# Two-layer hybrid decoder trunk on one core: mixer projections as one 512-column product per weight tile, with the halves added outside TensorE

## Chip, cores and metric

One core of one Trainium2 chip (trn2). The metric is device time in microseconds of one execution of the whole program. Engines are called by the profile's names: PE is TensorE, PEld its weight loads, DVE VectorE, ACT ScalarE, POOL GpSimd, SP SyncE.

## What is computed

Two layers over x of 256 tokens by 1024 channels, float32. Each layer has a token mixer and a retrieval sublayer (PEER), each followed by a LayerNorm. Only the mixer's projections of x are touched:

```
proj = x @ w_in                       # 1024 -> 12 pieces: aq ak av | lx lg | rq rk rv rg | ga gb gc
aq, ak = rope(aq), rope(ak)           # dilated softmax attention, 3 groups of 4 heads
lx -> short conv -> RG-LRU;  y_b = h * gelu(lg)
rq, rk = rope(rq), rope(rk)           # retention, 4 heads;  y_c = silu(rg) * norm(ret)
merged = sigmoid(ga) * (y_a @ wb_a) + sigmoid(gb) * (y_b @ wb_b) + sigmoid(gc) * (y_c @ wb_c)
x = LayerNorm(alpha * x + merged @ w_out);  x = LayerNorm(alpha * x + peer(x))
```

## The kernel before

Float32 products are made of parts: every operand is split into a high part (a cast to float32r) and a low part (the rest), and `high*high + high*low + low*high` is accumulated in PSUM. x stands transposed in SBUF as `xh` and `xl`, eight tiles of 128 channels by 256 tokens each.

The weights are one stream of 408 tiles (128x1024) a layer, called jobs. `run` takes them in order: for job i it splits the tile of job i+2 (`ensure_split`: SP loads `raw`, ACT casts `wh` at L250, DVE and for some jobs POOL subtract to get `wl` at L259), writes the job's products (`body`), lets each waiting side generator take a step (`pump`), and then writes the job's `post`. Each engine carries out its instructions in this written order. Three tiles of `wh` and `wl` exist, so the splitting can be two jobs ahead of PE and no more. `pool_cols` gives POOL 640 of the 1024 columns of `wl` in the first 12 attention jobs of a layer and 256 in the other 12.

A layer's jobs: 8 `lx`, 12 `av`, 24 `aq`/`ak`, 32 retention jobs (16 of them `rq`/`rk`), 8 `lg`, 16 for gate and branch b, 12 for a, 16 for c, 8 for the output projection; then 16, 128 and 128 jobs of PEER, which the change leaves alone.

A "T" job makes a transposed output: 128 output channels on the partitions, 256 tokens in the columns. `mm_t` (L301 to L308) writes for each of 8 channel tiles a product of `wh` with `xh` (L304) and with `xl` (L305), then 8 of `wl` with `xh` (L307): 24 products of 256 columns into half of a PSUM bank `mm` (2 buffers). Two T jobs fill a bank; the post of the second reads it. In attention and retention the reader is `rope_qk`: two DVE products of the PSUM bank with the rotary tables (L641, L642) into `w2` tiles (6 buffers), then a POOL subtraction and addition (L643, L644) into `qk`, which PE reads for the scores (L660, L754) two jobs later.

Beside the attention jobs run the side generators: `lru2` (DVE reciprocals L576, POOL products L577 and L578, later DVE L582 and L583), `scores` (PE L660, DVE L663) and `att` (softmax, transposes, products with v).

Of the kernel before, what the change touches and what calls it, by code (L numbers as in the profile page):

```python
# [11 lines left out]
F32 = mybir.dt.float32  # L12
F32R = mybir.dt.float32r
# [156 lines left out]
def build(ctx: ExitStack, tc: tile.TileContext, I, out, layers=LAYERS, dbg=None):  # L170
# [10 lines left out]
    par = cp.tile([P, LAYERS, 8, 12], F32, name="par")  # L181
    csp = cp.tile([P, LAYERS, 8], F32, name="csp")
    mhalf = cp.tile([P, 2], F32, name="mhalf")
    xh = cp.tile([P, KT, S], F32R, name="xh")
    xl = cp.tile([P, KT, S], F32R, name="xl")

    uid = [0]

    def nm(s):
        uid[0] += 1  # L190
        return f"{s}_{uid[0]}"

    def mmps():
        return ps.tile([P, 512], F32, tag="mm", name=nm("mm"), bufs=2)
# [322 lines left out]
    def mixer(l, mp, xdram, xnext):  # L517
# [9 lines left out]
        def w2():  # L527
            return mp.tile([P, 512], F32, tag="w2", name=nm("w2"), bufs=6)
# [59 lines left out]
        def body_lx(job, h, lo):  # L588
            ct = job[2]
            q = ct % 2  # L590
            if q == 0:
                V["p"] = mmps()
            pt = V["p"]
            (mm_t2 if ct == 0 else mm_t)(pt[:, q * S:(q + 1) * S], h, lo, xh, xl)
            for c, dst, src in ((0, wg, I["wgate"][l]), (2, rope, I["rope"]), (4, mask, I["mask"])):
                if c == ct:
                    nc.sync.dma_start(dst, src)

            def post():
                lx = w2()  # L600
                nc.scalar.copy(lx, pt)
                add_side("lru", lru1(ct // 2, lx))
                if ct == 7:
                    V["lru2"] = add_side("lru", lru2())
            return post if q else None
# [27 lines left out]
        run(take(12), body_av, 1.4)  # L633

        def rope_qk(pt, dst, c, s):
            src = pt.rearrange("p (a t) -> p a t", a=2)
            t1 = w2()
            t2 = w2()
            t1v = t1.rearrange("p (a t) -> p a t", a=2)
            t2v = t2.rearrange("p (a t) -> p a t", a=2)  # L640
            nc.vector.tensor_tensor(t1v, src, rope[:, c:c + 1, :].to_broadcast([P, 2, S]), op=ALU.mult)  # L641
            nc.vector.tensor_tensor(t2v, src, rope[:, s:s + 1, :].to_broadcast([P, 2, S]), op=ALU.mult)  # L642
            nc.gpsimd.tensor_tensor(dst[:, 0, :], t1[:, 0:S], t2[:, S:2 * S], op=ALU.subtract)  # L643
            nc.gpsimd.tensor_tensor(dst[:, 1, :], t2[:, 0:S], t1[:, S:2 * S], op=ALU.add)  # L644
# [76 lines left out]
        def body_att(job, h, lo):  # L721
            name, (g, p, part) = job[1], job[2]
            if part == 0:
                V["p"] = mmps()
            pt = V["p"]
            mm_t(pt[:, part * S:(part + 1) * S], h, lo, xh, xl)

            def post():
                k = int(name == "ak")
                if k == 0:  # L730
                    V["qk"] = mp.tile([P, 2, 2, S], F32, tag="qk", name=nm("qk"), bufs=2)
                rope_qk(pt, V["qk"][:, k], 0, 1)
# [56 lines left out]
        def body_ret(job, h, lo):  # L789
            name = job[1]  # L790
            if name in ("rv", "rg"):
                hp, k2 = job[2], job[3]
                if k2 == 0:
                    V["acc"] = accps2()
                acc = V["acc"]
                mm_n(acc, h, lo, xh, xl, k2, k2 == 3)

                def post_n():
                    a = mp.tile([P, 2, 512], F32, tag="r4", name=nm("r4"), bufs=5)
                    V[name] = a  # L800
                    for t in range(2):
                        if name == "rv":
                            nc.scalar.copy(a[:, t, :], acc[t])
                        else:
                            th = w2()
                            nc.scalar.activation(th, acc[t], AF.Tanh, scale=0.5)
                            nc.vector.scalar_tensor_tensor(a[:, t, :], th, 1.0, acc[t], op0=ALU.add, op1=ALU.mult)
                return post_n if k2 == 3 else None
            hd, part = divmod(job[2], 2)
            if part == 0:  # L810
                V["p"] = mmps()
            pt = V["p"]
            mm_t(pt[:, part * S:(part + 1) * S], h, lo, xh, xl)

            def post():
                k = int(name == "rk")
                if k == 0:
                    V["qk"] = mp.tile([P, 2, 2, S], F32, tag="qk", name=nm("qk"), bufs=2)
                rope_qk(pt, V["qk"][:, k], 2, 3)
                if k:  # L820
                    add_side("ret", ret(hd, V["qk"], V["rv"], V["rg"]))
            return post if part else None
# [7 lines left out]
        def body_lg(job, h, lo):  # L830
            ct = job[2]
            q = ct % 2
            if q == 0:
                V["p"] = mmps()
            pt = V["p"]
            mm_t(pt[:, q * S:(q + 1) * S], h, lo, xh, xl)

            def post():
                ge = w2()
                nc.scalar.activation(ge, pt, AF.Gelu)  # L840
                d = slice(ct - 1, ct + 1)
                hv = V["h"][:, d, :]
                nc.vector.tensor_tensor(hv, hv, ge.rearrange("p (a t) -> p a t", a=2), op=ALU.mult)
                split_from(ybh[:, d, :], ybl[:, d, :], hv)
            return post if q else None
# [6 lines left out]
        def body_bc(job, h, lo):  # L852
            dt = job[2]
            if job[0] == "T":
                V["p"] = mmps()
                mm_t(V["p"][:, 0:S], h, lo, xh, xl)
                return None
            b = job[1]
            pt = V["p"]
            yh, yl = (ybh, ybl) if b == "b" else (ych, ycl)  # L860
            mm_t(pt[:, S:2 * S], h, lo, yh, yl)

            def post():
                tg = mp.tile([P, S], F32, tag="tg", name=nm("tg"), bufs=2)
                nc.scalar.activation(tg, pt[:, 0:S], AF.Tanh, scale=0.5)
                if b == "b":
                    nc.vector.scalar_tensor_tensor(mg[:, dt, :], tg, 1.0, pt[:, S:2 * S], op0=ALU.add, op1=ALU.mult)
                    return
                nc.vector.scalar_tensor_tensor(tg, tg, 1.0, pt[:, S:2 * S], op0=ALU.add, op1=ALU.mult)
                nc.vector.tensor_tensor(mg[:, dt, :], mg[:, dt, :], tg, op=ALU.add)  # L870
                split_from(V["mh"][:, dt, :], V["ml"][:, dt, :], mg[:, dt, :])
            return post

        def body_a(job, h, lo):
            if job[0] == "T":
# [12 lines left out]
            for q in range(2):
                mm_t(pa[:, q * S:(q + 1) * S], h, lo, yaT[:, 0], yaT[:, 1], n=4, base=q * 512)

            def post():
                d = slice(2 * job[2], 2 * job[2] + 2)
                tmp = V["tga"]
                nc.vector.scalar_tensor_tensor(tmp, tmp, 1.0, pa, op0=ALU.add, op1=ALU.mult)
                nc.gpsimd.tensor_tensor(mg[:, d, :], mg[:, d, :], tmp.rearrange("p (a t) -> p a t", a=2), op=ALU.add)
            return post
# [396 lines left out]
```

## Time and profile before

| | us |
|---|---|
| median of 3 runs (2526.70 to 2528.17) | 2526.88 |
| the profiled execution | 2526.77 |
| its span, first to last instruction | 2524.9 |
| PE busy | 2481.4 (98%) |
| DVE busy | 1834.6 (73%) |
| ACT busy | 1177.1 (47%) |
| POOL busy | 283.0 (11%) |
| mean granted TensorE clock | 0.996 |

Shares are averages over stages that have different limits, so the stages are read one by one below. Matmuls are pipelined: a row's own duration (0.28 us for 256 columns) is longer than the distance to the next one, and what a product costs in a row of products is that distance. A wait of PE on a weight part shows under PEld or PE with the engine that released it.

### The profile page before, as it was taken

To read this page: it belongs to the slowest core of one execution; us is meant where nothing else is said; L and a number is where in the kernel's file an instruction comes from. 1 tells how busy PE (TensorE), PEld (TensorE's weight loads), DVE (VectorE), ACT (ScalarE), POOL (GpSimd) and SP (SyncE) were. 2 spreads that over 40 slices of the span, in tenths; PEclk is the share of its full clock that TensorE was granted. 3 is DMA by queue.
4 is the path that set the end of the run, shared out by engine and by line. 5 is a ranking of instruction groups with operands and counts; after the bars stand their busy time and mean duration, and the time that the engine had idled before them with its cause. 6 is when DMAs were issued, how large, how long until landed. Compare 5 with 4: busy or idle time off the path is not lost.

```text
span 2524.9 us, 43400 instructions
## 1 busy us (share of the span) xinstructions
PE 2481.4 (98%) x17428; PEld 2301.5 (91%) x17428; DVE 1834.6 (73%) x2736; ACT 1177.1 (47%) x1480; POOL 283.0 (11%) x263
## 2 busy tenths in 40 slices
PE   8999999999999999999999999999999999999998
PEld 8989999899999988888789899989999999888886
DVE  7876656889888856765588766568888888566655
ACT  5444444444544444444454444444454444444443
POOL 0821110200000000000028220102000000000001
PEclk9999999999999999999999999999999999999999
DMA  6445566555556658776554455655555666577664
GB/s 236 154 148 164 167 203 201 190 175 171 184 193 200 193 196 259 227 229 226 169 206 154 155 170 165 209 183 180 175 181 176 197 195 198 197 257 228 227 226 135
DMA packets 165913, 485.96 MB, mean 192 GB/s; under 512 B 15056, under 2 KB 47952, under 8 KB 165072
## 3 DMA queue, kind: packets, MB, share of 16 engines
q1 hardware_dynamic: 119952, 434.43, 52.5%
q10 hardware_dynamic: 44800, 45.62, 5.6%
q8 instruction: 137, 2.24, 0.4%
q0 software_dynamic: 960, 3.15, 0.3%
q14 instruction: 64, 0.52, 0.1%
HBM read 462.16 MB, written 20.97 MB: 191 GB/s over the span
## 4 chain that ended last, share of the span: by engine, by line
PE 93%; DVE 4%; issue 1%; POOL 1%; ACT 1%; ACTq 0%; POOLq 0%; DVEq 0%
PE acc L1202 27%; PE mm L304 17%; PE mm L307 17%; PE mm L305 17%; PE acc L334 2%; PE acc L335 2%; PE acc L338 2%; PE acc L1128 1%; DVE wl L259 1%; PE acc L1129 1%; PE side L660 1%; PE side L970 0%; POOL wl L259 0%; PE side L716 0%; PE side L709 0%
## 5 line engine op out<-in xcount | busy, mean ns | idle before, releaser
L259 DVE TENSOR_TENSOR wl<-raw,wh 128x1024 fp32r<-128x1024 f32 (+3 forms) x817 | 1002.6, 1232 | 475.7 <-ACT wh L250 470.9
L250 ACT CAST wh<-raw 128x1024 fp32r<-128x1024 f32 (+1 forms) x817 | 850.2, 1048 | 565.8 <-PE acc L1202 346.9
L304 PE MATMUL mm<-xh,wh 128*128 128x256 f32 x3536 | 880.5, 287 | 0.7 <-ACT wh L250 0.7
L305 PE MATMUL mm<-xl,wh 128*128 128x256 f32 x3536 | 868.5, 283 | 0.0
L304 PEld LDWEIGHTS mm<-xh,wh 128*128 128x128 f32 x3536 | 678.8, 192 | 3.3 <-issue 2.0
L305 PEld LDWEIGHTS mm<-xl,wh 128*128 128x128 f32 x3536 | 679.6, 192 | 0.5
L1202 PE MATMUL acc<-wh,act 128*128 128x512 f32 x2016 | 539.3, 389 | 0.9 <-ACT act L342 0.9
L307 PE MATMUL mm<-xh,wl 128*128 128x256 f32 x3536 | 497.6, 283 | 5.6 <-DVE wl L259 4.0
L307 PEld LDWEIGHTS mm<-xh,wl 128*128 128x128 f32 x3536 | 456.6, 192 | 6.8 <-DVE wl L259 4.4
L1202 PEld LDWEIGHTS acc<-wh,act 128*128 128x128 f32 x2016 | 378.2, 188 | 79.9 <-ACT act L342 1.4
L1202 PE MATMUL acc<-wl,act 128*128 128x512 f32 x1008 | 310.2, 389 | 0.0
L1202 PEld LDWEIGHTS acc<-wl,act 128*128 128x128 f32 x1008 | 189.2, 188 | 39.3
L1171 ACT ACTIVATE ring<-mm 128x512 f32<-128x512 f32 x128 | 76.5, 598 | 188.2 <-PE mm L307 175.5
L259 POOL TENSOR_TENSOR wl<-raw,wh 128x640 fp32r<-128x640 f32 (+2 forms) x50 | 68.8, 1386 | 725.6 <-ACT wh L250 681.4
L1098 ACT ACTIVATE ge<-acc 128x512 f32<-128x512 f32 x64 | 38.4, 600 | 164.1 <-PE acc L1129 164.1
L376 POOL TENSOR_TENSOR lnv<-lnv,mhalf 128x1 f32<-128x1 f32 x8 | 5.6, 697 | 770.7 <-DVE lnv L378 765.4
L334 PE MATMUL acc<-wh,xh 128*128 128x512 f32 x224 | 91.4, 408 | 0.0
L343 DVE TENSOR_TENSOR act<-ring,act 128x512 fp32r<-128x512 f32 x128 | 87.7, 685 | 1.4 <-ACT act L342 1.4
L335 PE MATMUL acc<-wh,xl 128*128 128x512 f32 x224 | 87.6, 391 | 0.0
L342 ACT CAST act<-ring 128x512 fp32r<-128x512 f32 x128 | 78.7, 615 | 5.0 <-DVE ring L1104 4.2
L643 POOL TENSOR_TENSOR qk<-w,w 128x256 f32<-128x256 f32 x40 | 51.4, 1284 | 183.5 <-DVE w L642 151.1
L338 PE MATMUL acc<-wl,xh 128*128 128x512 f32 x224 | 69.1, 390 | 0.0
(253 smaller groups left out, 2329.1 us busy)
## 6 DMA issues: line engine op xcount, KB each, us to landing
raw<-in_ws SPq DMA_DIRECT2D x815, 512.0 KB, 3.4
gd<-ge ACTq DMA_DIRECT2D x64, 256.0 KB, 3.3
ring<-gd ACTq DMA_DIRECT2D x8, 2048.0 KB, 15.7
wg<-in_wgate SPq DMA_DIRECT2D x2, 1024.0 KB, 5.8
kk<-in_keys ACTq DMA_DIRECT2D x2, 1024.0 KB, 5.4
xd<-L POOLq DMA_DIRECT2D x8, 256.0 KB, 2.8
X<-xd ACTq DMA_DIRECT2D x2, 1024.0 KB, 5.8
dec<-in_dec ACTq DMA_DIRECT2D x2, 768.0 KB, 4.4
```

Source lines behind the costliest of these rows:

```text
L250: nc.scalar.copy(h[:, c], raw[:, c])
L259: eng.tensor_tensor(lo[:, c], raw[:, c], h[:, c].bitcast(F32), op=ALU.subtract)
L304: mm(o, lhsT=w, rhs=mh[:, koff + k, :], start=(k == 0), stop=False)
L305: mm(o, lhsT=w, rhs=ml[:, koff + k, :], start=False, stop=False)
L307: mm(o, lhsT=lo[:, base + k * P:base + (k + 1) * P], rhs=mh[:, koff + k, :], start=False, stop=(k == n - 1))
L334: mm(acc[t], lhsT=sh[:, k, ts], rhs=h[:, q * 512:(q + 1) * 512], start=first, stop=False)
L335: mm(acc[t], lhsT=sl[:, k, ts], rhs=h[:, q * 512:(q + 1) * 512], start=False, stop=False)
L338: mm(acc[t], lhsT=sh[:, k, ts], rhs=lo[:, q * 512:(q + 1) * 512], start=False, stop=(last and q == 1))
L342: nc.scalar.copy(h, src)
L343: nc.vector.tensor_tensor(lo, src, h.bitcast(F32), op=ALU.subtract)
L1171: nc.scalar.activation(ring[s][:, i - 1:i + 1, :], pt.rearrange("p (a t) -> p a t", a=2), AF.Gelu)
L1202: mm(V["y"][t][n], lhsT=a[:, part, q, ts], rhs=w[:, n * 512:(n + 1) * 512], start=(j == 0 and x == 0), stop=False)
```

## The change

`xh` and `xl` become two halves of one tile `xx`, so that for each channel tile their 2 x 256 columns lie side by side. `mm_w` takes the place of `mm_t` in the T jobs of x (all but the first two `lx` jobs of a layer): 8 products of `wh` with 512 columns (high part of x in the first half of the output, low part in the second), then 8 of `wl` with 256 columns into the first half. The two halves of the output are added afterwards by `addhalves`: an ACT copy of the second half to SBUF (L325) and a DVE addition of the first half (L326). A pair of T jobs now takes a two-bank tile `acc`, which had been used by the "N" jobs alone (2 buffers). What had read PSUM now reads the sum in SBUF. For gates b and c the sum and the tanh are written in the T job's own post, and the branch product goes to a `side` bank.

```diff
-    xh = cp.tile([P, KT, S], F32R, name="xh")
-    xl = cp.tile([P, KT, S], F32R, name="xl")
+    xx = cp.tile([P, KT, 2, S], F32R, name="xx")
+    xh, xl = xx[:, :, 0, :], xx[:, :, 1, :]
...
+    def mm_w(o, h, lo, both, n=KT, base=0):
+        for k in range(n):
+            mm(o, lhsT=h[:, base + k * P:base + (k + 1) * P], rhs=both(k), start=(k == 0), stop=False)
+        for k in range(n):
+            mm(o[:, 0:S], lhsT=lo[:, base + k * P:base + (k + 1) * P], rhs=both(k)[:, 0, :], start=False,
+               stop=(k == n - 1))
+    def xboth(k):
+        return xx[:, k]
+    def addhalves(dst, pt):
+        v = pt.rearrange("p (a f t) -> p a f t", a=2, f=2)
+        nc.scalar.copy(dst, v[:, :, 1, :])
+        nc.vector.tensor_tensor(dst, dst, v[:, :, 0, :], op=ALU.add)
...
         def rope_qk(pt, dst, c, s):
-            src = pt.rearrange("p (a t) -> p a t", a=2)
+            src = w2().rearrange("p (a t) -> p a t", a=2)
+            addhalves(src, pt)
...
         def body_att(job, h, lo):
-                V["p"] = mmps()
+                V["p"] = accpair()
-            mm_t(pt[:, part * S:(part + 1) * S], h, lo, xh, xl)
+            mm_w(pt[:, part * 512:(part + 1) * 512], h, lo, xboth)
...
             def post():
                 ge = w2()
-                nc.scalar.activation(ge, pt, AF.Gelu)
+                addhalves(ge.rearrange("p (a t) -> p a t", a=2), pt)
+                nc.scalar.activation(ge, ge, AF.Gelu)
...
         def body_bc(job, h, lo):
             if job[0] == "T":
-                V["p"] = mmps()
-                mm_t(V["p"][:, 0:S], h, lo, xh, xl)
-                return None
+                pt = mmps()
+                mm_w(pt, h, lo, xboth)
+                def post_g():
+                    tg = mp.tile([P, S], F32, tag="tg", name=nm("tg"), bufs=3)
+                    nc.scalar.copy(tg, pt[:, S:512])
+                    nc.vector.tensor_tensor(tg, tg, pt[:, 0:S], op=ALU.add)
+                    nc.scalar.activation(tg, tg, AF.Tanh, scale=0.5)
+                    V["tg"] = tg
+                return post_g
-            pt = V["p"]
+            pt = sideps()[:, 0:S]
-            mm_t(pt[:, S:2 * S], h, lo, yh, yl)
+            mm_t(pt, h, lo, yh, yl)
```

The jobs of `lx` (from the third), `rq`/`rk`, `lg` and `ga` are changed like those of `aq`/`ak`. In the built program of both layers 1248 products of 512 columns and 1248 of 256 stand for 3744 of 256, that is for 156 jobs: 12 `lx`, 48 `aq`/`ak`, 32 `rq`/`rk`, 16 `lg`, 48 gates. DVE has 94 instructions more (62 of 512 columns, 32 of 256), ACT 88 more; POOL and SP have as many as before.

DVE in the attention stage of the first layer, before (`wl` are weight parts, L663 the scores, L641 and L642 the rotary products):

```order
L259 TENSOR_TENSOR wl_924<-raw_742,wh_923 128x384
L576 RECIPROCAL L_114_762<-L_114_762 128x256
L259 TENSOR_TENSOR wl_959<-raw_849,wh_958 128x384
L663 SCALAR_TENSOR_TENSOR sm_987<-side_989,mask_129 128x384
L663 SCALAR_TENSOR_TENSOR sm_988<-side_990,mask_129 128x384
L641 TENSOR_TENSOR w_148_1002<-mm_928,rope_128 128x512
L642 TENSOR_TENSOR w_149_1003<-mm_928,rope_128 128x512
L259 TENSOR_TENSOR wl_1011<-raw_884,wh_1010 128x384
```

The same place in the changed program:

```order
L259 TENSOR_TENSOR wl_852<-raw_757,wh_851 128x384
L594 RECIPROCAL L_114_716<-L_114_716 128x256
L259 TENSOR_TENSOR wl_879<-raw_790,wh_878 128x384
L688 SCALAR_TENSOR_TENSOR sm_899<-side_901,mask_128 128x384
L688 SCALAR_TENSOR_TENSOR sm_900<-side_902,mask_128 128x384
L326 TENSOR_TENSOR w_150_914<-w_150_914,acc_856 128x512
L666 TENSOR_TENSOR w_151_917<-w_150_914,rope_127 128x512
L667 TENSOR_TENSOR w_152_918<-w_150_914,rope_127 128x512
L259 TENSOR_TENSOR wl_926<-raw_817,wh_925 128x384
```

One addition stands ahead of the rotary products, and these read `w` (SBUF) where they read `mm` (PSUM).

DVE in gate and branch b, before (L867 multiplies the gate with the branch product):

```order
L259 TENSOR_TENSOR wl_3178<-raw_3075,wh_3177 128x1024
L259 TENSOR_TENSOR wl_3209<-raw_3111,wh_3208 128x1024
L867 SCALAR_TENSOR_TENSOR L_480_3110<-tg_3236,mm_3181 128x256
L259 TENSOR_TENSOR wl_3242<-raw_3142,wh_3241 128x1024
L259 TENSOR_TENSOR wl_3273<-raw_3175,wh_3272 128x1024
L867 SCALAR_TENSOR_TENSOR L_480_3110<-tg_3300,mm_3245 128x256
```

And in the changed program:

```order
L887 TENSOR_TENSOR tg_2890<-tg_2890,mm_2873 128x256
L259 TENSOR_TENSOR wl_2897<-raw_2808,wh_2896 128x1024
L899 SCALAR_TENSOR_TENSOR L_500_2748<-tg_2890,side_2900 128x256
L259 TENSOR_TENSOR wl_2929<-raw_2835,wh_2928 128x1024
L887 TENSOR_TENSOR tg_2949<-tg_2949,mm_2932 128x256
```

An addition of 256 columns (L887) stands between the weight parts of the T job and of the branch job.

## Rows read from the trace of the kernel before

**Rows 1.** The page, its parts 1 and 4: busy time of PE, and the chain that ended last by engine.

```profile
PE 2481.4 (98%) x17428; PEld 2301.5 (91%) x17428; DVE 1834.6 (73%) x2736; ACT 1177.1 (47%) x1480; POOL 283.0 (11%) x263
...
PE 93%; DVE 4%; issue 1%; POOL 1%; ACT 1%; ACTq 0%; POOLq 0%; DVEq 0%
```

**Rows 2.** Busy time by stretch (start:end, its length, then busy us and instructions of PE, PEld, DVE, ACT, POOL; granted clock; DMA). In order: the `lx` jobs, the attention jobs from the first L577 to the last third, the softmax part of attention, retention, `lg`, the gates and branches, all of layer 0; then `lx` and attention of layer 1.

```profile
5.75:34.09 28.34, 27.20 (x201) 26.49 (x202) 22.61 (x52) 15.78 (x23) 1.98 (x2) 1.00 0.88 316
79.64:120.86 41.22, 40.16 (x336) 38.02 (x335) 35.23 (x39) 14.31 (x14) 40.67 (x39) 1.00 0.49 162
120.86:143.90 23.04, 20.50 (x156) 19.96 (x155) 20.28 (x27) 10.93 (x17) 14.52 (x14) 0.93 0.44 145
...
158.44:268.38 109.94, 109.75 (x719) 98.50 (x717) 73.04 (x104) 45.94 (x63) 23.21 (x21) 1.00 0.49 161
268.38:294.84 26.46, 26.46 (x217) 26.20 (x215) 18.39 (x27) 14.89 (x21) 3.03 (x3) 1.00 0.44 139
294.84:420.92 126.08, 126.08 (x1059) 126.08 (x1057) 70.03 (x80) 55.50 (x72) 8.93 (x4) 1.00 0.62 202
1259.87:1290.66 30.79, 27.51 (x202) 25.39 (x202) 28.00 (x30) 17.14 (x27) 17.52 (x14) 0.99 0.62 229
1328.80:1412.63 83.83, 81.32 (x668) 78.42 (x666) 70.12 (x89) 35.84 (x45) 62.23 (x59) 1.00 0.47 158
```

**Rows 3.** Timeline of PE in an attention T job (start, length, what): its first product, its last eight, and the first of the next job.

```profile
98.85 0.28 PE L304 MATMUL mm<-xh,wh 128*128 128x256 f32 x1
...
100.77 1.12 PE L307 MATMUL mm<-xh,wl 128*128 128x256 f32 x8
101.73 0.28 PE L304 MATMUL mm<-xh,wh 128*128 128x256 f32 x1
```

**Rows 4.** Timeline of PE in PEER's last product: 512-column products in the same split form.

```profile
950.12 1.07 PE L1202 MATMUL acc<-wh,act 128*128 128x512 f32 x4
951.03 0.61 PE L1202 MATMUL acc<-wl,act 128*128 128x512 f32 x2
```

**Rows 5.** Timeline of POOL in the attention stage, one period of two jobs.

```profile
97.88 1.56 POOL L259 TENSOR_TENSOR wl<-raw,wh 128x640 fp32r<-128x640 f32 x1
99.41 1.05 POOL L577 TENSOR_TENSOR L<-L,L 128x256 f32<-128x256 f32 x1
100.55 0.74 POOL L578 TENSOR_TENSOR L<-L,L 128x256 f32<-128x256 f32 x1
101.25 1.88 POOL L259 TENSOR_TENSOR wl<-raw,wh 128x640 fp32r<-128x640 f32 x1
103.10 0.73 POOL L643 TENSOR_TENSOR qk<-w,w 128x256 f32<-128x256 f32 x1
103.80 1.05 POOL L644 TENSOR_TENSOR qk<-w,w 128x256 f32<-128x256 f32 x1
104.81 1.54 POOL L259 TENSOR_TENSOR wl<-raw,wh 128x640 fp32r<-128x640 f32 x1
```

**Rows 6.** Timeline of DVE at the same time.

```profile
98.21 1.65 DVE L259 TENSOR_TENSOR wl<-raw,wh 128x384 fp32r<-128x384 f32 x1
99.79 0.68 DVE L641 TENSOR_TENSOR w<-mm,rope 128x512 f32<-128x512 f32 x1
100.39 0.68 DVE L642 TENSOR_TENSOR w<-mm,rope 128x512 f32<-128x512 f32 x1
100.99 0.72 DVE L259 TENSOR_TENSOR wl<-raw,wh 128x384 fp32r<-128x384 f32 x1
...
103.29 0.96 DVE L259 TENSOR_TENSOR wl<-raw,wh 128x384 fp32r<-128x384 f32 x1
```

**Rows 7.** Groups of DVE by line and shape from 79.64 to 120.86 us (count, busy us, mean ns, idle before).

```profile
L259 DVE TENSOR_TENSOR wl<-raw,wh 128x384 fp32r<-128x384 f32 x9 | 9.9, 1096 | 0.5 <-ACT wh L250 0.5
...
L641 DVE TENSOR_TENSOR w<-mm,rope 128x512 f32<-128x512 f32 x7 | 4.8, 679 | 0.0
L642 DVE TENSOR_TENSOR w<-mm,rope 128x512 f32<-128x512 f32 x6 | 4.1, 677 | 0.0
```

**Rows 8.** The same from 172.8 to 200 us, where POOL is busy for a tenth of the time.

```profile
L259 DVE TENSOR_TENSOR wl<-raw,wh 128x1024 fp32r<-128x1024 f32 x8 | 9.8, 1221 | 3.7 <-ACT wh L250 3.6
...
L582 DVE SCALAR_TENSOR_TENSOR L<-L,L 128x256 f32<-128x256 f32 x2 | 0.8, 419 | 0.0
L641 DVE TENSOR_TENSOR w<-mm,rope 128x512 f32<-128x512 f32 x1 | 0.7, 689 | 0.0
...
L343 DVE TENSOR_TENSOR yaT<-side,yaT 128x256 fp32r<-128x256 f32 x1 | 0.4, 425 | 2.6 <-ACT yaT L342 2.6
```

**Rows 9.** The same from 120.86 to 158.44 us, with POOL busy about half of the time.

```profile
L582 DVE SCALAR_TENSOR_TENSOR L<-L,L 128x256 f32<-128x256 f32 x4 | 3.3, 820 | 0.0
```

**Rows 10.** Groups of ACT from 5 to 34 us: what a read of PSUM costs it.

```profile
L601 ACT COPY w<-mm 128x512 f32<-128x512 f32 x3 | 1.7, 582 | 2.7 <-PE mm L307 2.7
...
L558 ACT ACTIVATE w<-side,par 128x256 f32<-128x256 f32 x2 | 0.9, 475 | 4.7 <-PE side L556 4.7
```

**Rows 11.** Waits from 79.64 to 120.86 us (who, for whom: total us, times, longest).

```profile
ACT wh L250 <- PE mm L305: 14.8, 6, 4.2
...
PEld mm L307 <- POOL wl L259: 1.0, 2, 0.7
```

**Rows 12.** A stretch of two us behind the longest stop of PE in attention: length, PE busy, granted clock, DMA.

```profile
134.00:136.00 2.00, 1.73 (x8) 0.50 0.75 250
```

More of the change, by code (lines that the diff above doesn't have):

```diff
@@ L591, in body_lx @@
             if q == 0:
-                V["p"] = mmps()
+                V["p"] = mmps() if ct == 0 else accpair()
             pt = V["p"]
-            (mm_t2 if ct == 0 else mm_t)(pt[:, q * S:(q + 1) * S], h, lo, xh, xl)
+            if ct < 2:
+                (mm_t2 if ct == 0 else mm_t)(pt[:, q * S:(q + 1) * S], h, lo, xh, xl)
+            else:
+                mm_w(pt[:, q * 512:(q + 1) * 512], h, lo, xboth)
             for c, dst, src in ((0, wg, I["wgate"][l]), (2, rope, I["rope"]), (4, mask, I["mask"])):
@@ L600, in post @@
                 lx = w2()
-                nc.scalar.copy(lx, pt)
+                if ct < 2:
+                    nc.scalar.copy(lx, pt)
+                else:
+                    addhalves(lx.rearrange("p (a t) -> p a t", a=2), pt)
                 add_side("lru", lru1(ct // 2, lx))
@@ L810, in body_ret @@
             if part == 0:
-                V["p"] = mmps()
+                V["p"] = accpair()
             pt = V["p"]
-            mm_t(pt[:, part * S:(part + 1) * S], h, lo, xh, xl)
+            mm_w(pt[:, part * 512:(part + 1) * 512], h, lo, xboth)
             def post():
@@ L833, in body_lg @@
             if q == 0:
-                V["p"] = mmps()
+                V["p"] = accpair()
             pt = V["p"]
-            mm_t(pt[:, q * S:(q + 1) * S], h, lo, xh, xl)
+            mm_w(pt[:, q * 512:(q + 1) * 512], h, lo, xboth)
             def post():
                 ge = w2()
-                nc.scalar.activation(ge, pt, AF.Gelu)
+                addhalves(ge.rearrange("p (a t) -> p a t", a=2), pt)
+                nc.scalar.activation(ge, ge, AF.Gelu)
                 d = slice(ct - 1, ct + 1)
@@ L854, in body_bc @@
             if job[0] == "T":
-                V["p"] = mmps()
-                mm_t(V["p"][:, 0:S], h, lo, xh, xl)
-                return None
+                pt = mmps()
[7 more added lines that the diff above has]
+                return post_g
             b = job[1]
-            pt = V["p"]
+            pt = sideps()[:, 0:S]
             yh, yl = (ybh, ybl) if b == "b" else (ych, ycl)
-            mm_t(pt[:, S:2 * S], h, lo, yh, yl)
+            mm_t(pt, h, lo, yh, yl)
+            tg = V["tg"]
             def post():
-                tg = mp.tile([P, S], F32, tag="tg", name=nm("tg"), bufs=2)
-                nc.scalar.activation(tg, pt[:, 0:S], AF.Tanh, scale=0.5)
                 if b == "b":
-                    nc.vector.scalar_tensor_tensor(mg[:, dt, :], tg, 1.0, pt[:, S:2 * S], op0=ALU.add, op1=ALU.mult)
+                    nc.vector.scalar_tensor_tensor(mg[:, dt, :], tg, 1.0, pt, op0=ALU.add, op1=ALU.mult)
                     return
-                nc.vector.scalar_tensor_tensor(tg, tg, 1.0, pt[:, S:2 * S], op0=ALU.add, op1=ALU.mult)
+                nc.vector.scalar_tensor_tensor(tg, tg, 1.0, pt, op0=ALU.add, op1=ALU.mult)
                 nc.vector.tensor_tensor(mg[:, dt, :], mg[:, dt, :], tg, op=ALU.add)
@@ L877, in body_a @@
                 if dt % 2 == 0:
-                    V["pg"] = mmps()
+                    V["pg"] = accpair()
                 q = dt % 2
                 pt = V["pg"]
-                mm_t(pt[:, q * S:(q + 1) * S], h, lo, xh, xl)
+                mm_w(pt[:, q * 512:(q + 1) * 512], h, lo, xboth)
                 def post_g():
                     V["tga"] = w2()
-                    nc.scalar.activation(V["tga"], pt, AF.Tanh, scale=0.5)
+                    addhalves(V["tga"].rearrange("p (a t) -> p a t", a=2), pt)
+                    nc.scalar.activation(V["tga"], V["tga"], AF.Tanh, scale=0.5)
                 return post_g if q else None
```

## The prediction

> **What bounds the kernel now.** I read the page first, then busy time by stretch, then timelines of single engines. PE is busy for 98% of the span and holds 93% of the chain that ended last [rows 1], so time is mostly PE's. The stretches say where not [rows 2]. In `lg` and in the gates PE is busy all of the time, in retention 109.75 of 109.94 us, and DVE has some third of each free: PE alone bounds these. In the attention stretch from 79.64 to 120.86 us, PE is busy 40.16 of 41.22 us, but POOL is busy 40.67 us too and DVE 35.23: two engines are full at once, and a third nearly. In the softmax part DVE has 20.28 of 23.04 us and PE waits. In layer 1's `lx` DVE has 28.00 of 30.79 us.
>
> The reader is to see in the POOL timeline that it never rests: each row begins where the one before ended [rows 5]. One period of two jobs, from 97.88 to 104.81, takes 6.93 us: a weight part of 640 columns, L577, L578, a weight part, L643, L644. Where undisturbed, a 256-column row takes 0.73 and a 640-column one 1.54, so that the six sum to 2 x 1.54 + 4 x 0.73 = 6.0 us. The missing 0.9 us is in rows that are longer than their like (1.05 for 0.73, 1.88 for 1.54), each beside a DVE weight part. On DVE the same shows from the other side: the 384-column part that takes 0.72 at 100.99 takes 1.65 at 98.21 and ends 0.4 us after POOL's row does [rows 5, 6]. Two engines seem to pass one door in turn. Not every DVE row pays: the rotary products L641 and L642 take 679 and 677 ns in the POOL-full stretch and L641 689 ns where POOL is nearly idle [rows 7, 8]. L582, with two inputs in SBUF, takes 419 ns there and 820 on average beside POOL [rows 8, 9]. So DVE rows with two SBUF inputs pay beside POOL, rows with one input in PSUM do not.
>
> **PE, products.** 24 products of 256 columns lie 2.88 us apart from job to job, 0.120 us each (98.85 to 101.73, and eight of L307 from 100.77 to 101.73) [rows 3]. 512-column products of the same parts lie (951.03 - 950.12) / 4 = 0.2275 us apart [rows 4]. A changed job takes 8 x 0.2275 + 8 x 0.120 = 2.78 us, 0.10 less. 156 jobs: 15.6 us, 48 of them in attention (4.8), 12 in `lx` (1.2), 96 elsewhere (9.6). That is all that the change can give.
>
> A rule of the Trainium skill makes this smaller: "TensorE: Matmul & The Clock Gate", section "Back-to-back issue gap", gives columns / 2.4 + 2.5 ns for an isolated product, by which one of 512 saves 2.5 ns on two of 256, and the whole change 1248 x 2.5 ns = 3.1 us. The rows, 0.120 and 0.2275, are both above that formula, and their difference is the larger saving; I go by the rows.
>
> **ACT, copies.** 62 copies of 512 columns at 582 ns, six of them in place of copies that stood there, and 32 of 256 at no more than 475 ns [rows 10]: some 48 us in both layers. ACT has half of each stretch free [rows 2], so the work costs nothing; if that cover went, the weight casts behind it would come late. What counts is latency: about 0.6 us more between the last product and its reader.
>
> **DVE, additions.** 62 of 512 columns with one input in PSUM: 0.68 us each, as L641; 32 of 256 at 425 ns (L343) [rows 7, 8]. In the gates that is 13.6 us of 252 in two layers, with PE full and DVE at 70 of 126 us: nothing. In `lg`, ga and retention (2.7, 2.7 and 5.4 us a layer) nothing either. At the end of `lg`, copy and addition put 1.3 us before the branch input; the next T job's 2.78 us and the first half of the b job's products cover it. The tanh of gates b and c moves ahead of the branch product, out of the wait; no gain, as PE waited for neither.
>
> **Attention.** A rope pays three times on DVE: the addition (0.68, or 0.60 from start to start [rows 6]), and two products that now read two SBUF inputs. No row of before shows these. Bounds: nothing, as L641 beside POOL now; or a wait for a whole POOL row each, 0.73 to 1.54 us [rows 5]. At the lower bound the 12 additions of a layer (7.2 us) fit into DVE's rest. At the upper one, with 0.73, a rope takes 0.60 + 2 x 0.73 = 2.06 us on DVE, 24.7 us a layer, less the rest of 8.8 us (6.0 and 2.8 in the two stretches [rows 2]): 16 us. The nearest rows are the L259 and L582 ones, and I take their price: the door is held by each product for as long as its columns take, (1221 - 425) / 768 = 1.04 ns a column [rows 8], 0.53 us, 1.07 us a rope, and DVE waits 0.40 us each (820 - 419).
> - From 79.64 to 120.86: POOL has no rest, so what the door gives to DVE it takes from POOL, and with it from the weight parts that PE waits for (1.0 us already [rows 11]). Six ropes x 1.07 = 6.4 us. PE's own gain there is lost, since PE then waits.
> - From 120.86 to 143.90: POOL has rests, DVE is near full. Four ropes at 0.60 + 2 x 0.40 = 1.4 us: 5.6 us, less DVE's rest of 2.76: 2.8 us.
> - The last two ropes: 0.2 us gained on PE, as much lost; nothing.
>
> 9.2 us a layer. Layer 1's attention has about the same load (POOL 62.23 us, after 40.67 and 14.52 in layer 0's two stretches) [rows 2]: 18.4 us in both.
>
> "SBUF — State Buffer", section "Who interferes with whom", in the Trainium skill says that a VectorE instruction with two SBUF inputs contends with a GpSimd one that reads SBUF, that one with at most one does not, and that the later blocks until the earlier is through. The rows agree for L582 and L641; that it holds for a product with the broadcast rotary table, no run here shows. By it a whole POOL row can be waited out, which is the upper bound above.
>
> **`lx`.** Three additions a layer. Layer 0 has DVE rest (22.61 of 28.34) and PE's 0.6 us gain goes there: nothing. In layer 1, 3 x 0.68 = 2 us meet a rest of 2.79 us, part of it waits that cannot be moved: 1 us lost.
>
> **Sum.** -9.6 + 18.4 + 1.0 = +9.8 us on the profiled execution's own 2526.77 us: 2536.6. The median of the runs is 0.1 us above that execution; I say **2537 us**.
>
> **The rivals.**
> 1. *TensorE decides everywhere: faster.* In the POOL-full stretch ACT's casts still wait 14.8 us for PE [rows 11], so PE sets the pace there as well, and a part of POOL's busy time may be waiting. It decides if POOL can give up 1.07 us a rope without PE noticing. Against it: PE does wait for POOL's weight part [rows 11], and no POOL row starts late [rows 5]. Then all of 15.6 us come, or 9.6 with attention unchanged: 2511 to 2518 us.
> 2. *The losses only eat the gain: no change.* The door is taxed as said, but PE stops no more than 4 to 6 us a layer, since DVE's rest takes in the additions: -9.6 + 8 to 12 + 1: 2526 to 2531 us.
> 3. *The scores come late as well.* Before, L642 ended at 101.07 and POOL came to L643 at 103.10: 2.0 us to spare [rows 5, 6]. Copy (0.58), addition (0.60) and two waits (0.40 each) take 2.0 us. If it is more, POOL stands before L643 with the weight parts behind it, and PE before the scores. At 1.3 us for six scores a layer: 16 us more, 2553 us. A long stop also brings PE's clock down, as the half rate behind the softmax stop shows [rows 12].
> 4. *The wide product saves nothing*, if it takes as long as two narrow ones: 9.6 us less gain, 2546 us. [rows 4] speak against it with 512-column products of the same type.
>
> The formula of the clock-gate page above would put the saving near this case.
>
> **How the numbers follow.** Two levels count as different here when they are over 0.2% (5 us) apart, about what a measurement can tell. My forecast has 0.52: attention loses 6 to 16 us a layer (the upper bound), 2530 to 2550, nearly all of it slower. Rival 1 has 0.18, faster. Rival 2 has 0.15, and with a little of the forecast's lower end makes the middle 0.17. Rival 3 has 0.12 and rival 4 0.03, both slower. Slower: 0.65. The range leaves out rival 1 (0.18) and little else: it goes from 2520, between rivals 1 and 2, to 2555, behind rival 3.
>
> **What would show it.** The gate jobs 2.78 us apart where 2.88 stood, and the wide products 0.2275 apart (rival 4: 0.240). Rotary products of attention at about 1.0 us on average and the additions at 0.68 (rival 1: all 0.68). The attention stage some 9 us longer, with POOL without rest for longer and PE waiting for `wl` of POOL and DVE; retention, `lg` and gates 1.6, 0.8 and 2.4 us shorter. In rival 3, waits of POOL L643 on DVE inside the full stretch, and PE on `qk`. I would be wrong if attention kept its length, which would say that POOL's full row of instructions did not set PE's pace.

## The result: slower, by twice the forecast and for two reasons

| | before | changed |
|---|---|---|
| median of 6 runs, us | 2527.53 (2526.09 to 2528.41) | 2547.43 (2546.22 to 2550.84) |
| span of the profiled execution, us | 2524.9 | 2544.7 |

The ratio is 1.0081, 95% interval 1.0068 to 1.0094: 19.9 us slower. Forecast was slower, 2537 us, in a range from 2520 to 2555; the loss is twice the 9.8 us that the sum gave.

The page of the changed kernel, its parts 1 and 4, answers to [rows 1]:

```profile
PE 2483.3 (98%) x16180; PEld 2241.0 (88%) x16180; DVE 1906.6 (75%) x2830; ACT 1215.0 (48%) x1568; POOL 292.4 (11%) x263
...
PE 85%; DVE 7%; ACT 3%; POOL 2%; issue 2%; DMA 0%; ACTq 0%; SPq 0%; POOLq 0%; DVEq 0%
```

PE still looks busy for 98%, yet its part of the chain that ended last fell from 93% to 85%. Most of the 8 points went to DVE, ACT and POOL: PE waits for them, in stops that are mostly short (the longest new one, for softmax rows of DVE, has 4.2 us where 2.1 was the longest before).

Where they lie is told by the distance between the first products of the stages' first jobs, in both traces (layer 0, layer 1; us against before):

| stage | forecast, each layer | layer 0 | layer 1 |
|---|---|---|---|
| `lx` | 0, +1.0 | -0.3 | -0.2 |
| attention | +9.2 | +7.5 | +6.3 |
| retention | -1.6 | -0.9 | -0.9 |
| `lg` | -0.8 | +1.0 | +1.0 |
| gate and branch b | -0.8 | +0.8 | +0.8 |
| a | -0.8 | -0.7 | -0.7 |
| c | -0.8 | +1.4 | +1.4 |
| output projection | 0 | +1.9 | +1.0 |

All that follows is within 0.1 us. The last row is to be read with care: the output projections of the two layers differ by 0.46 us in the kernel before already, and by as much from run to run where nothing was changed near them. Attention lost less than was forecast; `lg`, b, c and the output projection, which were to gain 2.4 us a layer, lost 5.1 and 4.2. Busy time by stretch of the changed kernel, columns as in [rows 2]: the second half of attention, retention, `lg`, b, a, c, output projection of layer 0:

```profile
115.81:166.02 50.21, 44.52 (x252) 38.19 (x251) 45.65 (x56) 22.76 (x35) 30.42 (x30) 0.93 0.43 141
166.02:275.06 109.04, 108.75 (x591) 91.74 (x590) 79.11 (x112) 50.59 (x71) 25.30 (x21) 1.00 0.51 162
275.06:302.53 27.47, 26.48 (x152) 22.87 (x150) 20.10 (x30) 16.30 (x25) 3.06 (x3) 1.00 0.40 134
302.53:349.42 46.89, 46.02 (x320) 42.93 (x321) 28.01 (x36) 24.42 (x37) 0.00 (x0) 1.00 0.61 191
349.42:382.69 33.27, 33.27 (x227) 30.62 (x225) 21.81 (x20) 15.80 (x20) 6.62 (x3) 1.00 0.60 189
382.69:430.16 47.47, 46.41 (x323) 42.87 (x321) 29.59 (x45) 22.49 (x38) 2.21 (x1) 1.00 0.62 209
430.16:459.56 29.40, 26.59 (x112) 20.33 (x112) 20.87 (x30) 12.15 (x16) 1.35 (x2) 0.95 0.58 184
```

In c neither DVE (29.59 of 47.47) nor ACT (22.49) is near full, and PE is no longer busy all of the time. No share of busy time explains that loss; the written order does, as is shown below.

**Attention.** Groups of DVE from 80 to 129 us in the changed kernel, answering to [rows 7]:

```profile
L259 DVE TENSOR_TENSOR wl<-raw,wh 128x384 fp32r<-128x384 f32 x9 | 12.4, 1380 | 0.5 <-ACT wh L250 0.5
...
L666 DVE TENSOR_TENSOR w<-w,rope 128x512 f32<-128x512 f32 x7 | 8.3, 1193 | 0.2
L667 DVE TENSOR_TENSOR w<-w,rope 128x512 f32<-128x512 f32 x7 | 6.4, 916 | 0.0
...
L326 DVE TENSOR_TENSOR w<-w,acc 128x512 f32<-128x512 f32 x7 | 4.7, 674 | 0.0
```

The rotary products take 1193 and 916 ns where 679 and 677 stood; the addition, with one input in PSUM, takes 674. One such product on the timelines of DVE and POOL:

```profile
96.98 1.93 DVE L666 TENSOR_TENSOR w<-w,rope 128x512 f32<-128x512 f32 x1
```

```profile
96.79 1.57 POOL L259 TENSOR_TENSOR wl<-raw,wh 128x640 fp32r<-128x640 f32 x1
99.59 0.98 POOL L668 TENSOR_TENSOR qk<-w,w 128x256 f32<-128x256 f32 x1 [1.23 <-DVE w L667]
```

The DVE row begins 0.19 us after POOL's and ends at 98.91, 0.55 us after POOL's end at 98.36. From POOL's end on it has about the time that such a product needs from start to start (0.60 [rows 6]), as if it had been let in when POOL was through. POOL's next row then waits 1.23 us for the second product, a rest that it did not have before. In retention, where POOL is busy for 25.30 of 109.04 us, the same two products with the same inputs take 0.69 us, so it is not the second SBUF input by itself that makes them long:

```profile
L666 DVE TENSOR_TENSOR w<-w,rope 128x512 f32<-128x512 f32 x8 | 5.5, 692 | 0.5
L667 DVE TENSOR_TENSOR w<-w,rope 128x512 f32<-128x512 f32 x8 | 5.5, 685 | 0.0
```

The first twelve attention jobs of layer 0, before and changed, columns as in [rows 2]:

```profile
72.25:112.08 39.83, 38.77 (x322) 37.14 (x321) 35.30 (x41) 17.17 (x17) 35.49 (x32) 1.00 0.45 151
```

```profile
72.30:115.81 43.51, 38.89 (x225) 32.34 (x224) 42.88 (x45) 18.87 (x21) 35.48 (x30) 1.00 0.41 134
```

DVE is full now (42.88 of 43.51 us), and POOL is busy no longer than before. Waits from 80 to 129 us, beside those from 79.64 to 120.86 in [rows 11]:

```profile
PEld acc L316 <- POOL wl L259: 5.4, 6, 1.6
POOL qk L668 <- DVE w L667: 4.9, 4, 1.2
...
PEld side L685 <- POOL qk L668: 1.8, 3, 1.1
```

**Gates.** ACT and DVE in gate and branch c of the changed kernel, one pair of jobs:

```profile
402.95 0.41 ACT L360 CAST L<-L 128x256 fp32r<-128x256 f32 x1 [2.15 <-DVE L L902]
403.26 1.04 ACT L250 CAST wh<-raw 128x1024 fp32r<-128x1024 f32 x1
404.21 0.36 ACT L886 COPY tg<-mm 128x256 f32<-128x256 f32 x1
405.92 0.42 ACT L888 ACTIVATE tg<-tg 128x256 f32<-128x256 f32 x1 [1.35 <-DVE tg L887]
406.25 1.03 ACT L250 CAST wh<-raw 128x1024 fp32r<-128x1024 f32 x1
409.36 0.41 ACT L360 CAST L<-L 128x256 fp32r<-128x256 f32 x1 [2.08 <-DVE L L902]
```

```profile
404.33 1.23 DVE L259 TENSOR_TENSOR wl<-raw,wh 128x1024 fp32r<-128x1024 f32 x1 [0.52 <-ACT wh L250]
405.47 0.41 DVE L887 TENSOR_TENSOR tg<-tg,mm 128x256 f32<-128x256 f32 x1
407.31 1.23 DVE L259 TENSOR_TENSOR wl<-raw,wh 128x1024 fp32r<-128x1024 f32 x1 [1.42 <-ACT wh L250]
408.45 0.41 DVE L901 SCALAR_TENSOR_TENSOR tg<-tg,side 128x256 f32<-128x256 f32 x1
408.90 0.43 DVE L902 TENSOR_TENSOR L<-L,tg 128x256 f32<-128x256 f32 x1
```

Read them as one line that passes between two engines: cast (ACT, 403.26), its weight part (DVE, 404.33), the addition written behind that (405.47), the tanh that needs the addition (ACT, 405.92), the next cast written behind the tanh (406.25), its weight part (407.31), the gate product and the sum behind that (408.45, 408.90), the split of the sum (ACT, 409.36), and the next cast. Each row starts about when the one before ends, on the other engine or behind it on the same one. The round takes 409.36 - 402.95 = 6.41 us a pair. PE needs 5.67, the distance of the first wide products of two pairs:

```profile
399.70 2.00 PE L314 MATMUL mm<-xx,wh 128*128 128x512 f32 x8
...
405.37 2.00 PE L314 MATMUL mm<-xx,wh 128*128 128x512 f32 x8
```

The splitting is up to two jobs ahead of PE, and this lead covers the missing 0.74 us a pair for a while: five pairs of c lie 5.67 us apart. Then the lead is used up, PE waits for casts, and the last three pairs take 6.21, 6.42 and 6.49 us. PE enters the output projection with no lead left. ACT is idle for half of the stage and DVE for over a third of it, each waiting for the other. PE's wait for the casts of c, among the waits from 382.69 to 459.56 us:

```profile
PE mm L314 <- ACT wh L250: 0.7, 2, 0.4
```

Branch b is another case: its first pair takes 7.18 us and each of the other seven 5.67. All that b lost, it lost behind the end of `lg`.

### The profile page after: what moved, and what is told of

Its sections match the earlier page's. It is cut to its first block, busy times and chain, and to the rows that moved or that the text cites. A ratio compares the mean times of both kernels' runs of the same rounds, so it can differ in the third digit from the quotient of the medians.

```text
span 2544.7 us, 41061 instructions
## 1 busy us (share of the span) xinstructions
PE 2483.3 (98%) x16180; PEld 2241.0 (88%) x16180; DVE 1906.6 (75%) x2830; ACT 1215.0 (48%) x1568; POOL 292.4 (11%) x263
## 4 chain that ended last, share of the span: by engine, by line
PE 85%; DVE 7%; ACT 3%; POOL 2%; issue 2%; DMA 0%; ACTq 0%; SPq 0%; POOLq 0%; DVEq 0%
PE acc L1235 27%; PE mm L304 11%; PE mm L307 11%; PE mm L305 11%; PE acc L314 6%; PE acc L316 3%; DVE wl L259 3%; PE acc L356 2%; PE acc L352 2%; PE acc L353 2%; ACT wh L250 2%; PE acc L1161 1%; PE acc L1162 1%; PE mm L314 1%; POOL wl L259 1%
## 5 line engine op out<-in xcount | busy, mean ns | idle before, releaser
L259 DVE TENSOR_TENSOR wl<-raw,wh 128x1024 fp32r<-128x1024 f32 (+3 forms) x817 | 1014.3, 1246 | 469.6 <-ACT wh L250 465.6
L304 PE MATMUL mm<-xx,wh 128*128 128x256 f32 x2288 | 568.1, 286 | 0.0
L305 PE MATMUL mm<-xx,wh 128*128 128x256 f32 x2288 | 561.3, 283 | 0.0
L305 PEld LDWEIGHTS mm<-xx,wh 128*128 128x128 f32 x2288 | 439.3, 192 | 0.0
L304 PEld LDWEIGHTS mm<-xx,wh 128*128 128x128 f32 x2288 | 438.8, 192 | 0.0
L307 PE MATMUL mm<-xx,wl 128*128 128x256 f32 x2288 | 321.9, 283 | 4.0 <-DVE wl L259 4.0
L307 PEld LDWEIGHTS mm<-xx,wl 128*128 128x128 f32 x2288 | 295.9, 192 | 4.4 <-DVE wl L259 4.4
L314 PE MATMUL acc<-xx,wh 128*128 128x512 f32 x992 | 258.1, 403 | 0.8 <-ACT wh L250 0.8
L314 PEld LDWEIGHTS acc<-xx,wh 128*128 128x128 f32 x992 | 181.7, 191 | 37.0 <-ACT wh L250 1.7
L316 PEld LDWEIGHTS acc<-xx,wl 128*128 128x128 f32 x992 | 136.5, 191 | 17.8 <-POOL wl L259 7.6
L316 PE MATMUL acc<-xx,wl 128*128 128x256 f32 x992 | 140.5, 283 | 6.2 <-POOL wl L259 6.2
L352 PE MATMUL acc<-wh,xx 128*128 128x512 f32 x224 | 91.4, 408 | 0.0
```

What stands on the lines that cost most here:

```text
L259: eng.tensor_tensor(lo[:, c], raw[:, c], h[:, c].bitcast(F32), op=ALU.subtract)
L314: mm(o, lhsT=h[:, base + k * P:base + (k + 1) * P], rhs=both(k), start=(k == 0), stop=False)
L316: mm(o[:, 0:S], lhsT=lo[:, base + k * P:base + (k + 1) * P], rhs=both(k)[:, 0, :], start=False, stop=(k == n - 1))
L352: mm(acc[t], lhsT=sh[:, k, ts], rhs=h[:, q * 512:(q + 1) * 512], start=first, stop=False)
```

## Experiments

The theory for attention is the **port**: DVE's rotary products now have two SBUF inputs and take turns with POOL. Its rival is **serial**: the addition and the hand-off from ACT to DVE alone make the loss. The theory for `lg` and the gates is the **round**: the written order makes ACT and DVE wait for each other. Its rivals are work (too much of it), or the end of `lg` alone. Ratios are to the kernel before, with their intervals.

**1. The sum goes back to PSUM.** Only in `rope_qk`:

```diff
-            src = w2().rearrange("p (a t) -> p a t", a=2)
-            addhalves(src, pt)
+            low = w2().rearrange("p (a t) -> p a t", a=2)
+            halves = pt.rearrange("p (a f t) -> p a f t", a=2, f=2)
+            src = halves[:, :, 0, :]
+            nc.scalar.copy(low, halves[:, :, 1, :])
+            nc.vector.tensor_tensor(src, low, src, op=ALU.add)
```

> The changed kernel, except that rope_qk writes the sum of the halves back to PSUM, so that both rotary products read one input in PSUM and one in SBUF. DVE and ACT keep the same number of instructions. Port theory (the loss in attention, 7.5 and 6.3 us in the two layers, is POOL and DVE taking turns at the second SBUF read): rotary products of attention back at 0.68 us each, attention loses some 3 us a layer less, total 2539 to 2541 against 2547 of the changed kernel. Rival, serial theory (the loss is the added addition and the hand-off ACT to DVE): attention keeps its length within 1 us, total 2546 to 2548.

Measured: 2538.32 us, 1.004 (1.0027 to 1.0054), 9.1 us less than the changed kernel. Attention is 1.0 and 3.0 us longer than before where the changed kernel's was 7.5 and 6.3. DVE from 80 to 129 us:

```profile
L669 DVE TENSOR_TENSOR w<-acc,rope 128x512 f32<-128x512 f32 x7 | 4.8, 692 | 0.2
L664 DVE TENSOR_TENSOR acc<-w,acc 128x512 f32<-128x512 f32 x7 | 4.8, 683 | 0.0
L670 DVE TENSOR_TENSOR w<-acc,rope 128x512 f32<-128x512 f32 x7 | 4.8, 681 | 0.0
```

The same number of instructions, all near 0.68 us. The first half of attention, where POOL does not rest, is back within 0.04 and 0.3 us of its length before. DVE is busy for 39.25 of 39.88 us of it in layer 0: the additions just fit. The serial rival is left the 1.0 and 3.0 us, which lie in the softmax half; in layer 1 the granted clock is lower there as well (0.96, before 1.00).

**2. The gates' posts, late.** Copy, addition and tanh of gates b and c are written with the branch job:

```diff
-                def post_g():
-                    tg = mp.tile([P, S], F32, tag="tg", name=nm("tg"), bufs=3)
-                    nc.scalar.copy(tg, pt[:, S:512])
-                    nc.vector.tensor_tensor(tg, tg, pt[:, 0:S], op=ALU.add)
-                    nc.scalar.activation(tg, tg, AF.Tanh, scale=0.5)
-                    V["tg"] = tg
-                return post_g
+                V["pgate"] = pt
+                return None
             b = job[1]
+            gp = V["pgate"]
...
             def post():
+                tg = mp.tile([P, S], F32, tag="tg", name=nm("tg"), bufs=3)
+                nc.scalar.copy(tg, gp[:, S:512])
+                nc.vector.tensor_tensor(tg, tg, gp[:, 0:S], op=ALU.add)
+                nc.scalar.activation(tg, tg, AF.Tanh, scale=0.5)
```

> The changed kernel, except that copy, addition and tanh of gates b and c are written in the post of the branch job instead of the gate's own. The work of every engine is the same. Ring theory (in gates b and c casts, weight parts, additions and tanh of ACT and DVE wait for each other in turn, 6.41 us a pair where TensorE needs 5.67): gates b and c each 0.8 us a layer shorter than before the change instead of 0.8 and 1.4 longer, the output projection back to its length, total about 2537. Rival, work theory (ACT and DVE have too much to do, or the branch product's bank comes free late): the stages keep their lengths, total 2547.

Measured: 2541.43 us, 1.0056 (1.0043 to 1.007), 6.0 us less than the changed kernel. c is 0.69 us shorter than before the change in each layer where it had been 1.4 longer, the output projection 0.5 and 0.0 us longer where it had been 1.9 and 1.0. b stays 0.81 us longer, against the expectation, and the total is 4 us above the expected one. ACT in c:

```profile
400.94 0.41 ACT L360 CAST L<-L 128x256 fp32r<-128x256 f32 x1 [1.02 <-DVE L L901]
401.25 2.00 ACT L250 CAST wh<-raw 128x1024 fp32r<-128x1024 f32 x2
403.15 0.36 ACT L894 COPY tg<-mm 128x256 f32<-128x256 f32 x1
405.06 0.42 ACT L896 ACTIVATE tg<-tg 128x256 f32<-128x256 f32 x1 [1.55 <-DVE tg L895]
406.42 0.41 ACT L360 CAST L<-L 128x256 fp32r<-128x256 f32 x1 [0.95 <-DVE L L901]
```

The two casts of a pair stand together again, so that one hand-over for a weight part falls out of the round: 5.48 us from split to split, less than PE's 5.67. All eight pairs of c take 5.67 us, and PE is full:

```profile
382.43:427.80 45.37, 45.37 (x322) 42.70 (x321) 33.36 (x47) 24.07 (x40) 2.21 (x1) 1.00 0.69 227
```

Same work, other order: work is out for c. What b lost is not in its gates' order; its first pair still takes 7.18 us.

**3. Attention as before**, with narrow products and rotary products from PSUM for `aq` and `ak`:

```diff
-                V["p"] = accpair()
+                V["p"] = mmps()
-            mm_w(pt[:, part * 512:(part + 1) * 512], h, lo, xboth)
+            mm_t(pt[:, part * S:(part + 1) * S], h, lo, xh, xl)
...
-                rope_qk(pt, V["qk"][:, k], 0, 1)
+                rope_qk(pt, V["qk"][:, k], 0, 1, True)
...
+            if whole:
+                src = pt.rearrange("p (a t) -> p a t", a=2)
```

> The changed kernel with the 48 aq and ak jobs as before the change (narrow products, rotary products from PSUM), retention still changed. If the stages add up: attention back to 86.2 and 83.8 us, total 2547.4 - 13.9 = 2533.5. If retention or the later stages inherited delays from attention, lower than that, 2530.

Measured: 2533.78 us, 1.0025 (1.0016 to 1.0034). Attention is within 0.2 us of before in both layers, every other stage within some 0.5 us of the changed kernel's, but `lx` (0.5 and 1.0 us longer than before). The stages add up; nothing behind attention inherits its delay.

**4. The port and a copy alone.** The kernel before, whose rotary products now read a copy in SBUF:

```diff
-            src = pt.rearrange("p (a t) -> p a t", a=2)
+            sb = w2()
+            nc.scalar.copy(sb, pt)
+            src = sb.rearrange("p (a t) -> p a t", a=2)
```

> The kernel before, with one thing of the change alone: an ACT copy of the PSUM pair to SBUF ahead of the rotary products, which then read two SBUF inputs. No wide products, no addition on DVE. Port theory: rotary products beside POOL at 0.9 to 1.2 us, attention 5 to 7 us a layer longer, total 2537 to 2541 against 2527.5. Serial theory: a copy on an engine that is half idle, 2527 to 2529.

Measured: 2538.02 us, 1.0041 (1.0028 to 1.0055), 10.5 us slower without a single wide product or addition. Attention is 5.8 and 5.1 us longer, retention as long as before. DVE from 80 to 129 us:

```profile
L644 DVE TENSOR_TENSOR w<-w,rope 128x512 f32<-128x512 f32 x7 | 9.7, 1384 | 0.0
L643 DVE TENSOR_TENSOR w<-w,rope 128x512 f32<-128x512 f32 x7 | 9.1, 1294 | 0.0
```

The same two products, the same columns, twice as long. The run holds ACT's copy too, and the wait for it; run 1 has the same copy and loses little, so the copy is not what costs here. With run 1 this settles attention: 5.8 and 5.1 us for the port with the copy, 1.0 and 3.0 for copy, addition and wide products without the port, 7.5 and 6.3 for all. PE's waits in the whole trace (us) say in which way each of them acts:

| PE waits for | before | changed | run 1 | run 4 |
|---|---|---|---|---|
| weight parts of POOL | 1.4 | 6.2 | 2.1 | 5.1 |
| `qk` of POOL | 1.1 | 3.8 | 1.2 | 5.5 |
| softmax rows of DVE | 3.0 | 6.5 | 6.6 | 4.4 |

Without the port the waits for POOL are nearly back to where they were; the wait for the softmax stays, as DVE still has the additions.

**5. Wide products where they cost nothing.** Run 2's kernel with `lx`, `aq`, `ak` and `lg` as before the change (edits as in run 3).

> The wide products only in rq and rk, ga and (with the posts of the second run) gates b and c; lx, aq, ak and lg as before the change. If the losses of the stages are their own (ports in attention, hand-offs in lg, DVE's full row in lx): retention 0.93, ga 0.68, gates b and c 0.69 each a layer shorter than before the change, all else as before, total 2527.5 - 6.0 = 2521.5. Rival: gate b's loss of 0.81 in the second run belongs to gate b and not to lg: 2524.5.

Measured: 2521.4 us, 0.9978 (0.9969 to 0.9987): faster than both kernels. Retention is 0.9 and 1.0, b, a and c 0.67 to 0.69 us shorter each, all as expected, b too: with `lg` as before, b's loss is gone. As b kept its loss with attention as before (run 3), it was `lg`'s. PE in b now:

```profile
294.37:339.75 45.38, 45.38 (x322) 42.70 (x321) 26.77 (x34) 22.99 (x35) 0.00 (x0) 1.00 0.60 200
```

**6. `lg`'s hand-offs apart.** Run 2's kernel, with gelu, product and split of a pair of jobs (`rest`) written behind the next job; the last pair's stay where they were:

```diff
+            def rest(ge, d):
                 nc.scalar.activation(ge, ge, AF.Gelu)
...
+            def post():
+                if q:
+                    ge = w2()
+                    addhalves(ge.rearrange("p (a t) -> p a t", a=2), pt)
+                    V["rest"] = (ge, slice(ct - 1, ct + 1))
+                    if ct < 7:
+                        return
+                if V.get("rest"):
+                    rest(*V.pop("rest"))
-            return post if q else None
+            return post
```

> The second run's kernel (gates b and c late, all else as changed), and in lg gelu, product and split of a pair are written one job later than copy and addition, except for the last pair. Same work. Hand-off theory: the round of casts, weight parts, copy, addition, gelu, product and split (5.99 us a pair where TensorE needs 5.55) falls apart, lg 0.7 us shorter than before the change instead of 1.0 longer, gate b less than 0.8 longer; total 2541.4 - 3 to 5 = 2536.5 to 2538.5. Rival, the end of lg alone (the last pair's chain to the branch input): lg and gate b together stay within 0.5 us, 2541.

Measured: 2536.88 us, 1.004 (1.0027 to 1.0054), 4.6 us less than run 2. `lg` is 0.61 and 0.63 us shorter than before the change where it had been 1.0 longer. In the changed kernel ACT had stood up to 3.54 us before a gelu, since the addition that it needs came behind a weight part and retention's last normalisation on DVE, and the next cast stood behind that gelu. Now PE is busy throughout:

```profile
274.56:300.41 25.85, 25.85 (x153) 22.84 (x151) 20.76 (x30) 16.77 (x25) 3.05 (x3) 1.00 0.44 150
```

b is 0.2 us longer than before, not 0.7 shorter. So of run 2's 0.81 us in b, 0.6 went with the round in `lg`. The 0.9 us that are still missing from b's gain all lie in its first pair, 6.57 us where the other seven take 5.67:

```profile
300.41 2.00 PE L314 MATMUL mm<-xx,wh 128*128 128x512 f32 x8
...
305.56 0.39 PE L305 MATMUL side<-L,wh 128*128 128x256 f32 x1 [0.34 <-DVE L L361]
...
306.98 2.00 PE L314 MATMUL mm<-xx,wh 128*128 128x512 f32 x8
```

PE stands there before the branch input, for the split of `lg`'s last pair: that pair's copy, addition, gelu, product and split are not covered. No run moved that chain by itself.

**7. `lx` added to run 5.** The edits of the change in `lx`, else run 5.

> As the fifth run's kernel, but with lx changed too (six jobs a layer wide, three additions more on DVE). If the 1.0 us that lx of layer 1 lost in the first three runs is lx's own: 1.0 us more than the fifth run, layer 0 within 0.5. Rival, PE's gain counts: 1.2 us less.

Measured: 2521.43 us, 0.9975 (0.9966 to 0.9984), no different from run 5. Layer 1's `lx` is 1.0 us longer than before and layer 0's 0.1, as expected; a microsecond is below what these runs can tell in total. The stage shows it, as in runs 1, 2, 3 and 6 (1.0 each); the changed kernel's own trace does not (-0.2). The sixth job tells why, in run 7 and in the changed kernel:

```profile
1278.11:1283.34 5.23, 5.23 (x22) 4.35 (x21) 5.12 (x9) 2.26 (x4) 0.86 (x2) 0.67 0.71 267
```

```profile
1291.77:1295.84 4.07, 3.92 (x22) 3.27 (x21) 3.96 (x7) 2.26 (x4) 0.85 (x2) 1.00 0.60 189
```

The granted clock is 0.67 in the one and 1.00 in the other, behind a stretch of 2.9 us in which PE was busy for 0.9 in both. In each of the five traces with the 1.0 us the clock is at the half rate (0.50) for a part of that job. So the microsecond came with the clock and not from the time of three additions, which the changed kernel has too. Why the clock did not fall there in the changed kernel is open.

## Why the prediction was right, and where it was not

**The port: right, a third too large.** The sign of attention's loss came from it, and runs 1 and 4 show it. Rotary products at about 1.0 us on average were forecast, 1.05 came. The term was 9.2 us a layer; 7.5 and 6.3 were measured, of which the port's part is 6.5 and 3.4 by what run 1 took away, and 5.8 and 5.1 by run 4. In the POOL-full half I charged 1.07 us for each of six ropes, 6.4 us; that half lost 3.7 and 5.1 us, the latter with a granted clock of 0.93. The way was in part another: the text let POOL pay for what the port gives to DVE. In layer 0's half POOL was busy as long as before (35.48 and 35.49 us) and waited for DVE, which had become full; in layer 1's both grew (POOL from 35.99 to 38.58 us, DVE from 33.62 to 43.06). The Trainium skill's rule in "SBUF — State Buffer", section "Who interferes with whom", that the ports which VectorE and GpSimd share are an exclusive lock, agrees with the row of 1.93 us beside POOL's 1.57 us, here for a product with the broadcast rotary table; that one SBUF input is free of it agrees with run 1's 692 and 681 ns.

**The failed step.** The text said of ACT's copies "the work costs nothing", of the additions in the gates and `lg` "nothing", and of the tanh that moves ahead "no gain, as PE waited for neither". It priced work by busy shares and a latency at the end of `lg`. It did not follow the written order round: what stands behind the tanh on ACT is the next cast, behind that cast's weight part on DVE the gate product and the sum, behind these the split and one more cast on ACT, and behind that cast's part the addition that the next tanh needs. Runs 2 and 6 show that the same instructions in another order give c 2.1 us a layer back and `lg` 1.6. By the table of stages the miss is 9.6 us (19.4 measured, 9.8 forecast): `lg`, b, c and the output projection make 14.1 of it (2.4 a layer forecast as gained, 5.1 and 4.2 lost), retention 1.4, a 0.2, attention -4.6 and `lx` -1.5. The second step that failed is the end of `lg`: the text had its chain covered by the next T job and half of the b job. In the changed kernel b's first pair takes 7.18 us for 5.67, so 1.5 us a layer were not covered, and 0.9 in run 6. That 2547 us lies inside the stated range owes something to luck: the upper part of the range was there for attention and late scores, not for `lg` and the gates, and the attention term was 4.6 us too large, while `lg`, b, c and the output projection came out 14.1 us worse than forecast.

**`lx`: not shown.** The microsecond of layer 1 did not come in the changed kernel (-0.2), and in the runs that have it, it came with the clock.

**Products: right, a little small.** The saving of 0.10 us a job came out at 0.69 / 8 = 0.086 in the gates and 0.9 / 16 = 0.06 in retention. There one job is 0.3 us longer than before (4.39 for 4.11), as PE waits 0.5 us for the last `qk` of POOL. The wide products lie 0.229 us apart in c ((2.00 - 0.40) / 7, with 0.40 us for one), where [rows 4] gave 0.2275; "TensorE: Matmul & The Clock Gate" in the Trainium skill, section "Back-to-back issue gap", gives 0.216 for an isolated product, by which an estimated 0.02 us a job would be saved; the traces here show four times that in the gates.

**Rivals.** TensorE decides everywhere (0.18): no, it waits in attention, `lg`, b and c. Losses only eat the gain (0.15): in attention alone nearly so, in total no. Scores come late (0.12): partly there: from 80 to 129 us PE waits 1.8 us for `qk` of POOL's L668, and POOL 4.9 us for DVE, but within the port's loss. Wide products save nothing (0.03): no.

## What to carry to other kernels

Moving an operand of a VectorE product from PSUM to SBUF can cost more than the wider TensorE products give, where GpSimd has no rest: look for two full engines side by side, and leave the sum in PSUM. Where two partly idle engines run in written order, a hand-over added between them is not priced by their shares: write down the round from one weight tile to the next over both, add it up, and compare it with what the bounding engine needs. A change that is made at every place can be right at half of them; stage by stage, this one is worth 5.4 us.

## What the runs showed that was not expected

The price of the port is no constant a product. In the changed kernel, where an addition from PSUM stands ahead of them, the two rotary products average 1.05 us, 0.36 over the 0.69 that they take in retention; in run 4, with the same two inputs and no addition ahead, 1.34 us, 0.65 over it. Where DVE is full, its time in all counts: with the addition a rope takes 2.78 us on DVE in the changed kernel and 2.68 in run 4, DVE is busy for 42.88 and 42.78 us of layer 0's first half, and that half takes 43.51 and 43.23 us. In run 1 a rope takes 2.06 us, DVE is busy for 39.25 us, and the half keeps its length. In layer 1's first half DVE is not full in run 4 (40.16 of 44.07 us); what sets the pace there is not shown.

And the busy shares hid the gates' loss: c lost 1.4 us with ACT busy 22.49 and DVE 29.59 of 47.47 us, and PE at 46.41, which reads as 98%.
